# Attention on one core: part of the turning of probabilities by DMA, a paced TensorE order, and paired low products

## The chip, the cores and the metric

The kernel runs on one core of one Trainium2 chip, in one launch. The metric is the time of that launch on the device in microseconds (us), the median of several runs; less is better.

## The reference, cut to what matters

A trunk of two layers over 2048 tokens of width 1024, batch 1, in float32: a Mamba-2 mixer, then multi-head latent attention (16 heads; queries and keys of 64 + 32 columns, values of 64), then a final norm. The change touches the attention:

```python
for i in range(S // Q_BLOCK):                       # 16 query tiles of 128
    q0 = i * Q_BLOCK
    kv_len = q0 + Q_BLOCK
    s = einsum('bqhd,bkhd->bhqk', q_nope[:, q0:kv_len], k_nope[:, :kv_len]) + \
        einsum('bqhr,bkr->bhqk', q_rope[:, q0:kv_len], k_rope[:, :kv_len])
    mask = (q0 + local)[:, None] >= arange(kv_len)[None, :]
    p = softmax(where(mask, s * scale, -inf), axis=-1)
    outs.append(einsum('bhqk,bkhd->bqhd', p, v[:, :kv_len]))
```

The query and its scale, the shared keys and values, the gate and the output projection are computed around it.

## The kernel before

The kernel works in stages: the Mamba layer and the projections for the attention (to about 2127 us of the profiled execution), the attention (`heads`, to about 3050 us), and the gate, output projection and final norm (`back`, to the end). To keep float32's precision, a matrix is split into a high and a low part and multiplied in several passes: `mm3` (lines 84 to 87) is three TensorE passes, high by high, high by low, low by high.

**Attention.** The work is a list of 64 jobs, 16 heads by 4 blocks of 512 queries (`qb`, called block below). A block has four query tiles `j` of 128. For a query tile, `scores` cuts the keys up to the diagonal into chunks of at most 512 (`cuts`), so a tile of block 3 has four chunks. One chunk is one score step: `mm3` into a bank of PSUM (tag "mm", four banks), on the last chunk the mask (line 905), then VectorE's maximum of the bank (line 906). When all chunks of the tile are there, line 910 makes the negative row maximum `nm`, and ScalarE takes the exponential of each bank into a tile `Pr` in SBUF, with the row sum (line 918). The exponentials are held back in a list `late`: one is issued ahead of each following score step, and each frees a score bank. The two parts of all scores of a head are 40 chunks.

**Turning and values.** The value product needs the probabilities with the keys on the partitions. A unit is one key tile of 128 keys against the 512 queries of a block. `turn` transposes its four 128x128 squares on TensorE (line 933) into a bank with tag "tr", and `pair16` (lines 116 and 117) takes the bank, scaled by `PSCALE`, into a 16-bit high part (ScalarE) and a 16-bit low part (VectorE), both in a tile `PTs`. `values` multiplies them with the values (lines 943 and 944): the value tile has 128 columns, 64 of high parts and 64 of low ones, so both products give 64 rows of high and 64 of low, which `finish` adds when it stores them: rows 0 to 63 are written to `o_d` by SP's queue and rows 64 to 127 added by POOL's. On the diagonal, units are narrower (512, 384, 256 and 128 queries).

**Order.** TensorE's order in `heads` is the order in which the code issues it (a manual schedule). After the first `LAG` = 20 score steps, each score step is followed by the turns (T) and value products (V) that a hand-written table `CREDIT` gives for its block, query tile and chunk. The other engines' orders are made by the scheduler when the kernel is built, and each engine then works through its own queue in order; POOL's queue holds the loads of queries, keys and values (lines 833 to 847) and the accumulating stores (line 956), SP's holds the plain stores (line 952).

**Memory.** `Pr` has 24 buffers. The loads of a later head's queries and values wait for a buffer of the tag "xT". `back` prepares its output weights per step k (line 1016 a rounded copy on ScalarE, line 1017 the remainder on POOL); for k = 2 to 5 they have memory of their own, so that this is done while the attention still runs.

Of the kernel before, what the change touches and what calls it, by code (L numbers as in the profile page):

```python
# [40 lines left out]
LAG = 20  # L41
DEPTH = 2
CREDIT = (
    (("VT",), ("TV",), ("VT",), ("TV",)),
    (("", "VTVT"), ("", "TTVV"), ("", "TTVV"), ("", "TTVV")),
    (("TT", "", "VVTV"), ("TV", "", "VTTV"), ("TV", "", "TTVV"), ("TTV", "", "TVV")),
    (("T", "", "", "VVTTVTV"), ("T", "V", "", "VTTVTV"), ("T", "V", "V", "TVTTV"), ("TV", "V", "", "TVTVT")),
)
MAGIC = 12582912.0
PSCALE = 32768.0  # L50
# [18 lines left out]
class Net:  # L69
# [44 lines left out]
    def pair16(self, hi, lo, src, scale=1.0):  # L114

        self.nc.scalar.activation(hi, src, AF.Copy, scale=scale)  # L116
        self.nc.vector.scalar_tensor_tensor(lo, src, scale, hi, ALU.mult, ALU.subtract)  # L117
# [146 lines left out]
    def value_scale(self):  # L264
# [4 lines left out]
        for n in range(2):  # L269
# [18 lines left out]
            v.tensor_scalar(e, e, -25, None, ALU.add)  # L288
# [574 lines left out]
    def heads(self, sp):  # L863
        nc, v = self.nc, self.nc.vector
        begun = []
        keys, vals, quer = self.keys, self.vals, self.quer

        def cuts(kv):

            out, at = [], 0  # L870
            while at < kv:
                w = min(TB, kv - at)
                if kv - at == TB + P:
                    w = 384
                out.append((at, max(w, 256)))
                at += w
            return out

        def scores(h, qb, st):
# [8 lines left out]
            for j in range(4):  # L888
# [3 lines left out]
                mx = self.t(sp, "mx", [P, 4], bufs=4)  # L892
                banks = []
                for n, (c0, w) in enumerate(parts):
# [6 lines left out]
                    if n == nb - 1:  # L901
                        if qb == j == 0:
# [3 lines left out]
                    v.tensor_reduce(mx[:, n:n + 1], s[:, :w], AX.X, ALU.max)  # L906
                    banks.append((s, w))
                    yield CREDIT[qb][j][n]
                nm = self.t(sp, "nm", [P, 1], bufs=4)
                v.tensor_reduce(nm, mx[:, :nb], AX.X, ALU.max, negate=True)  # L910
# [4 lines left out]
                def exp(n, j=j, nb=nb, parts=parts, banks=banks, nm=nm, p=p, sm=sm):  # L915
                    s, w = banks[n]
                    x = self.t(sp, "Pr", [P, TB], bufs=NP)
                    nc.scalar.activation(x[:, :w], s[:, :w], AF.Exp, bias=nm, accum_out=sm[:, n:n + 1])  # L918
                    for c in range(0, w, P):
                        p[(parts[n][0] + c) // P] = x[:, c:c + P]  # L920
# [7 lines left out]
        def turn(h, qb, kb, st):  # L928
# [6 lines left out]
            u = self.t(sp, "PTs", [P, 2, TB], F16, bufs=5)  # L935
            self.pair16(u[:, 0, c], u[:, 1, c], pt[:, c], PSCALE)
            return u[:, :, c], c

        def values(h, qb, kb, st, u, c):
            if kb == 0:  # L940
                st["O"] = self.t(self.pp, "tr", [P, TB], bufs=4)
            nk = 4 * qb + 4
            nc.tensor.matmul(st["O"][:, c], vals[h][:, kb, :], u[:, 0], start=kb == 0, stop=False)  # L943
            nc.tensor.matmul(st["O"][:, c], vals[h][:, kb, :], u[:, 1], start=False, stop=kb == nk - 1)  # L944
            if kb == nk - 1:
# [22 lines left out]
        states = [{"P": []} for _ in jobs]  # L968
        sums = {}
        def ahead():  # L970
            for n, (h, qb) in enumerate(jobs):
                if qb == 0:
                    sums[h] = self.t(sp, "sum", [P, 16], bufs=3)
                yield from scores(h, qb, states[n])

        units = [(h, qb, kb, states[n]) for n, (h, qb) in enumerate(jobs) for kb in range(4 * qb + 4)]
        held = []

        def work(what):

            if what == "T" and units:
                a = units.pop(0)
                held.append((a, turn(*a)))
            elif what == "V" and held and (len(held) > DEPTH or not units):
                a, (u, c) = held.pop(0)
                values(*a, u, c)

        step = 0
        for credit in ahead():
            step += 1  # L990
            if step > LAG:
                for what in credit:
                    work(what)
        while units or held:
            work("T")
            work("V")
# [193 lines left out]
```

## Time and profile before

| | |
|---|---|
| median of 3 runs | 3239.51 us (3238.54 to 3240.34) |
| the profiled execution, its own time | 3238.15 us |
| its span (first to last instruction) | 3236.3 us |
| TensorE busy | 3156.2 us, 98% of the span |
| VectorE (DVE) busy | 2593.4 us, 80% |
| ScalarE (ACT) busy | 2055.2 us, 64% |
| GpSimd (POOL) busy | 646.2 us, 20% |
| mean granted TensorE clock | 0.995 |

The times of single instructions come from one profiled execution. Busy time counts the stretches in which an engine has an instruction on record; records of neighbours overlap by a little (a pipeline's tail), so an instruction's mean time is longer than the distance to the next one. PE is TensorE, PEld its weight load. In the profile's groups, "L117 DVE ... PTs<-tr,PTs" is line 117 on VectorE, writing tile PTs from tiles tr and PTs, with shapes, count, total and mean time, and the engine's idle time just ahead, with what ended it. The chain of waits follows the end back to what released each step; its pieces are a start, a time and a step, and "x8" means eight instructions merged.

### The profile page before, as it was taken

The page shows a single profiled execution, that of the slowest core. Times are in us where ns is not written, and L with a number is a line of the kernel's source. Part 1 is how long each engine was busy: PE and PEld are TensorE (multiplying, and loading weights), DVE is VectorE, ACT ScalarE, POOL GpSimd, SP SyncE. Part 2 cuts the span into 40 slices and gives each one's busy share as a digit, 9 for nine tenths or more (in the row PEclk, how much of TensorE's full clock was granted, in tenths as well). Part 3 has the DMA queues.
Part 4 walks back from the last instruction along what each step waited for, and adds up shares of the span by engine and source line. Part 5 has one row for each costly group of instructions (what it writes and reads, how often), then busy time and mean ns, then how long its engine had stood idle before and what let it go on. Part 6 is the DMA issues. An engine that isn't in the chain of part 4 may idle for free.

```text
span 3236.3 us, 50476 instructions
## 1 busy us (share of the span) xinstructions
PE 3156.2 (98%) x16708; PEld 2563.4 (79%) x16708; DVE 2593.4 (80%) x5490; ACT 2055.2 (64%) x5117; POOL 646.2 (20%) x842
## 2 busy tenths in 40 slices
PE   8999999999999999998999999999999999999998
PEld 6788888888888888887888888777777777777787
DVE  6988888889889888887776765668888888888675
ACT  5666666666657655666555554567777877778522
POOL 1221122221212222222211211222212212223100
PEclk9999999999999999999999999999999999999999
DMA  5333343333433334333466666753443434344385
GB/s 174 108 104 92 118 131 119 105 96 122 140 96 109 90 125 145 104 94 111 132 221 212 236 204 208 246 137 79 82 89 77 97 77 88 77 90 116 81 272 172
DMA packets 210572, 418.91 MB, mean 129 GB/s; under 512 B 27107, under 2 KB 68835, under 8 KB 208869
## 3 DMA queue, kind: packets, MB, share of 16 engines
q1 hardware_dynamic: 168900, 291.39, 28.9%
q0 software_dynamic: 41408, 124.29, 15.7%
q8 instruction: 132, 2.16, 0.3%
q14 instruction: 132, 1.07, 0.1%
HBM read 321.33 MB, written 94.24 MB: 128 GB/s over the span
## 4 chain that ended last, share of the span: by engine, by line
PE 44%; ACT 3%; DMA 2%; DVE 2%; issue 1%; SPq 0%; POOL 0%; ACTq 0%; DVEq 0%
PE mm L85 7%; PE mm L87 7%; PE mm L86 7%; PE tr L933 6%; PE tr L943 3%; PE tr L944 3%; PE tr L86 3%; PE tr L87 3%; PE tr L85 3%; ACT Pr L918 1%; DVE PTs L117 1%; ACT PTs L116 1%; DMA wraw<-in_kv_w_up_dram 1%; PE mm L905 1%; DMA wraw<-in_kv_w_down_dram 0%
## 5 line engine op out<-in xcount | busy, mean ns | idle before, releaser
L117 DVE SCALAR_TENSOR_TENSOR PTs<-tr,PTs 128x512 f16<-128x512 f32 (+3 forms) x640 | 374.7, 607 | 92.6 <-ACT PTs L116 86.0
L116 ACT ACTIVATE PTs<-tr 128x512 f16<-128x512 f32 (+3 forms) x640 | 328.2, 541 | 140.9 <-PE tr L933 140.0
L906 DVE TENSOR_REDUCE mx<-mm 128x1 f32<-128x512 f32 (+2 forms) x631 | 375.5, 607 | 45.4 <-PE mm L87 42.8
L918 ACT ACTIVATE Pr<-mm,nm 128x512 f32<-128x512 f32 (+2 forms) x631 | 395.1, 635 | 23.1 <-DVE nm L910 21.5
L108 ACT ACTIVATE wsp<-wraw 128x512 fp32r<-128x512 f32 (+1 forms) x452 | 251.1, 574 | 171.7 <-PE mm L87 82.4
L109 DVE TENSOR_TENSOR wsp<-wraw,wsp 128x512 fp32r<-128x512 f32 (+1 forms) x452 | 301.8, 680 | 69.7 <-ACT wsp L108 68.9
L85 PE MATMUL mm<-xT,wsp 128*128 128x512 f32 x800 | 321.0, 401 | 0.0
L933 PE MATMUL tr<-pack,Pr 128*128 128x128 f32 x2176 | 317.5, 273 | 0.9 <-ACT Os L950 0.8
L87 PE MATMUL mm<-xT,wsp 128*128 128x512 f32 x800 | 314.1, 393 | 0.0
L86 PE MATMUL mm<-xT,wsp 128*128 128x512 f32 x800 | 312.9, 391 | 0.0
L85 PE MATMUL mm<-K,xT 96*128 96x512 f32 (+2 forms) x639 | 286.7, 449 | 23.1 <-ACT Pr L918 21.7
L933 PEld LDWEIGHTS tr<-pack,Pr 128*128 128x128 f32 x2176 | 253.4, 141 | 49.3 <-ACT Os L950 1.6
L85 PE MATMUL mm<-wsp,xT 128*128 128x512 f32 (+1 forms) x640 | 242.1, 378 | 0.0
L86 PE MATMUL mm<-wsp,xT 128*128 128x512 f32 (+1 forms) x640 | 237.7, 371 | 0.0
L87 PE MATMUL mm<-wsp,xT 128*128 128x512 f32 (+1 forms) x640 | 237.5, 372 | 0.0
L87 PE MATMUL mm<-K,xT 96*128 96x512 f32 (+2 forms) x639 | 231.4, 362 | 0.0
L358 DVE SCALAR_TENSOR_TENSOR cacc<-craw,pack,cacc 128x512 f32<-128x512 f32 x288 | 216.5, 774 | 18.3 <-ACT cacc L356 17.8
L86 PE MATMUL mm<-K,xT 96*128 96x512 f32 (+2 forms) x639 | 231.1, 362 | 0.0
L496 POOL TENSOR_TENSOR Xp<-Xw,Xp 128x512 fp32r<-128x512 f32 x64 | 83.1, 1298 | 697.5 <-ACT Xp L495 393.1
L943 PE MATMUL tr<-PTs,xT 128*128 128x512 f16 (+3 forms) x640 | 222.0, 348 | 0.1
L538 ACT ACTIVATE Xw<-tr,d_wend 128x64 f32<-128x64 f32 x512 | 182.8, 358 | 58.7 <-DVE Xd L534 58.6
L944 PE MATMUL tr<-PTs,xT 128*128 128x512 f16 (+3 forms) x640 | 219.4, 347 | 0.0
(368 smaller groups left out, 8145.9 us busy)
## 6 DMA issues: line engine op xcount, KB each, us to landing
wraw<-in_ssm_w_in_dram SPq DMA_DIRECT2D x256, 256.0 KB, 2.8
big<-cumT SPq DMA_DIRECT2D x64, 512.0 KB, 4.0
wraw<-in_ssm_w_out_dram SPq DMA_DIRECT2D x128, 256.0 KB, 2.6
wraw<-in_ssm_w_in_dram SPq DMA_DIRECT2D x129, 128.0 KB, 2.2
xT<-qn_d POOLq DMA_DIRECT2D x64, 256.0 KB, 4.4
K<-kn_d POOLq DMA_DIRECT2D x15, 1024.0 KB, 9.2
wraw<-in_mla_w_uq_dram SPq DMA_DIRECT2D x36, 256.0 KB, 4.0
hx<-in_x_dram SPq DMA_DIRECT2D x16, 512.0 KB, 4.2
```

Source lines behind the costliest of these rows:

```text
L85: mm(out, l_hi, r_hi, start=start, stop=False)
L86: mm(out, l_hi, r_lo, start=False, stop=False)
L87: mm(out, l_lo, r_hi, start=False, stop=stop)
L108: nc.scalar.activation(hi, src, AF.Copy)
L109: nc.vector.tensor_tensor(lo, src, hi.bitcast(F32), ALU.subtract)
L116: self.nc.scalar.activation(hi, src, AF.Copy, scale=scale)
L117: self.nc.vector.scalar_tensor_tensor(lo, src, scale, hi, ALU.mult, ALU.subtract)
L906: v.tensor_reduce(mx[:, n:n + 1], s[:, :w], AX.X, ALU.max)
L918: nc.scalar.activation(x[:, :w], s[:, :w], AF.Exp, bias=nm, accum_out=sm[:, n:n + 1])
L933: nc.tensor.transpose(pt[:, j * P:(j + 1) * P], st["P"][j][kb], self.ident)
L943: nc.tensor.matmul(st["O"][:, c], vals[h][:, kb, :], u[:, 0], start=kb == 0, stop=False)
L944: nc.tensor.matmul(st["O"][:, c], vals[h][:, kb, :], u[:, 1], start=False, stop=kb == nk - 1)
```

## The change

- **Turning by DMA.** In blocks 1, 2 and 3 the first 1, 1 and 2 chunks of keys (`BYDMA`), all off the diagonal, aren't turned on TensorE. After the exponential, VectorE casts the 128x512 chunk to 16 bits, POOL subtracts for the low part, both into a tile `Ph` (four buffers), and SP issues one transposing DMA of the 128x1024 elements into `PX` (five buffers), from where the value products read.
- **Scale.** The factor 32768 goes into the exponential's bias (`PSHIFT` is its logarithm), and out of `pair16`, whose subtraction becomes a plain one. The maxima are taken negated, and `nm` is a running minimum: 28 small steps a head in place of 16. The first query tile of block 1 is cut 512 + 256, with a wider mask, in place of 384 + 256.
- **Low products.** `values` issues only the product with the high part. The low parts are collected, and `lows` multiplies four key tiles at a time: each with the 64 high columns of the values alone, key tiles in turn into rows 0 to 63 and 64 to 127 of the same bank.
- **Order.** `CREDIT` is replaced: each score step earns time for other work by its columns, 85% of it kept until the last chunk of a query tile, and `action` spends it by set prices. A job's turns and values start no sooner than `GAP` = 5 score steps after its last one; within a job, units turned by DMA and by TensorE are interleaved.
- **Memory.** The output weights of k = 2 to 5 move from their own pool into the pool of `back`, which lies where the attention's tiles were.

```diff
+BYDMA = (0, 1, 1, 2)
+T_US, V_US, S_US = 0.436, 0.216, 0.7
+L_US = 0.45
...
-    def pair16(self, hi, lo, src, scale=1.0):
-
-        self.nc.scalar.activation(hi, src, AF.Copy, scale=scale)
-        self.nc.vector.scalar_tensor_tensor(lo, src, scale, hi, ALU.mult, ALU.subtract)
+    def pair16(self, hi, lo, src):
+
+        self.nc.scalar.activation(hi, src, AF.Copy)
+        self.nc.vector.tensor_tensor(lo, src, hi, ALU.subtract)
...
-                    v.tensor_reduce(mx[:, n:n + 1], s[:, :w], AX.X, ALU.max)
+                    m = mx[:, n:n + 1]
+                    v.tensor_reduce(m, s[:, :w], AX.X, ALU.max, negate=True)
...
+                    if nb == 1:
+                        v.tensor_scalar(nm, m, PSHIFT, None, ALU.add)
+                    elif n == 1:
+                        v.scalar_tensor_tensor(nm, m, mx[:, 0:1], shift, ALU.min, ALU.add)
+                    elif n > 1:
+                        v.scalar_tensor_tensor(nm, m, shift, old, ALU.add, ALU.min)
...
                     nc.scalar.activation(x[:, :w], s[:, :w], AF.Exp, bias=nm, accum_out=sm[:, n:n + 1])
+                    if n < BYDMA[qb]:
+
+                        u = self.t(sp, "Ph", [P, 2, TB], F16, bufs=4)
+                        v.tensor_copy(u[:, 0], x)
+                        nc.gpsimd.tensor_tensor(u[:, 1], x, u[:, 0], ALU.subtract)
+                        if j == 0:
+                            st["X"].append(self.t(sp, "PX", [P, 2, 4, TB], F16, bufs=5))
+                        d = st["X"][n].rearrange("p s k q -> p (s k) q")[:, :, j * P:(j + 1) * P]
+                        nc.sync.dma_start_transpose(d, u.rearrange("p s k -> p (s k)"))
...
-            u = self.t(sp, "PTs", [P, 2, TB], F16, bufs=5)
-            self.pair16(u[:, 0, c], u[:, 1, c], pt[:, c], PSCALE)
+            hi, lo = self.t(sp, "PTh", [P, TB], F16, bufs=5), self.t(sp, "PTl", [P, TB], F16, bufs=10)
+            self.pair16(hi[:, c], lo[:, c], pt[:, c])
...
-            nc.tensor.matmul(st["O"][:, c], vals[h][:, kb, :], u[:, 0], start=kb == 0, stop=False)
-            nc.tensor.matmul(st["O"][:, c], vals[h][:, kb, :], u[:, 1], start=False, stop=kb == nk - 1)
+            nc.tensor.matmul(st["O"][:, c], vals[h][:, kb, :], u[0], start=not st["done"], stop=False)
+            st["done"] += 1
+            st["lo"].append((kb, u[1], c))
+
+        def lows(h, qb, st):
...
+            for i, (kb, l, c) in enumerate(st["lo"]):
+                d = slice(i % 2 * 64, i % 2 * 64 + 64)
+                nc.tensor.matmul(st["O"][d, c], vals[h][:, kb, 0:64], l, start=False, stop=end and i >= n - 2)
...
+            if owed and (len(owed[0][2]["lo"]) >= 4 or owed[0][2]["done"] == 4 * owed[0][1] + 4):
...
+                lows(h, qb, st)
+                return L_US * pairs
...
+            if turns and turns[0][0] < limit and (len(turned) <= DEPTH or not ready):
+                b = turns.pop(0)[1]
+                turned[b[:3]] = turn(*b)
+                return T_US * (4 - max(b[2] - 4 * b[1], 0)) / 4
...
+            limit = max([k + 1 for k in ended if k < n and ended[k] + GAP <= step], default=0)
+            if step <= LAG:
+                continue
+            share = 1.06 * rate * w
+            kept += share if last else share * 0.85
+            if last:
+                allowed, kept = allowed + kept, 0.0
+            else:
+                allowed += share * 0.15
+            while allowed > 0:
+                t = action(limit)
+                if not t:
+                    allowed = min(allowed, 2.0)
+                    break
+                allowed -= t
...
-                    W.append(self.t(self.wo, "W", [P, 2, 2, TB], F32R, bufs=4))
+                    W.append(self.t(sp, "W", [P, 2, 2, TB], F32R, bufs=4))
```

More of the change, by code (lines that the diff above doesn't have):

```diff
@@ L988, in heads, with order @@
-        step = 0
-        for credit in ahead():
-            step += 1
[L991 to L996, printed above, removed]
+                for step in scores(h, qb, states[n]):
+                    yield (n, *step)
+        def order(qb):
+            d, p = list(range(4 * BYDMA[qb])), list(range(4 * BYDMA[qb], 4 * qb + 4))
+            return sorted(d + p, key=lambda kb: kb / len(d) if kb in d else (kb - len(d) + 0.5) / len(p))
```

80 lines of the change are left out of this document (51 added, 29 removed).

## The prediction

> **What bounds the kernel now.** I read the page's first part first, then windows over the attention, then who waited for whom there, then the chain of waits, and last single groups by shape.
>
> ```profile
> PE 3156.2 (98%) x16708; PEld 2563.4 (79%) x16708; DVE 2593.4 (80%) x5490; ACT 2055.2 (64%) x5117; POOL 646.2 (20%) x842
> ```
>
> TensorE is busy 98% of the span, so only work taken off it, or idle time put on it, moves the end. The change lies in the attention. The window here starts and ends at the same instruction of the same step, 13 heads apart.
>
> ```profile
> core 0: us, PE busy (x) PEld busy (x) DVE busy (x) ACT busy (x) POOL busy (x), PEclk, DMA share, GB/s
> 2180.50:2922.00 741.50, 724.94 (x4589) 556.98 (x4587) 624.01 (x1483) 586.82 (x1625) 156.36 (x247) 1.00 0.43 85
> ```
>
> Divided by 13, one head takes 57.04 us: PE busy 55.8, DVE 48.0, ACT 45.1, POOL 12.0, the DMA engines 0.43 x 57.04 = 24.5. PE is the bound, idle 1.3 us a head, and the clock is full. DVE is only 8 us behind it.
>
> ```profile
> POOL xT L845 <- PE tr L962: 187.2, 14, 13.6
> ACT PTs L116 <- PE tr L933: 126.5, 126, 2.3
> DVE mx L906 <- PE mm L87: 35.5, 69, 1.2
> PE mm L85 <- ACT Pr L918: 17.7, 17, 1.2
> ```
>
> PE waits for one thing only: a score bank that the exponential has not yet emptied (17.7 us in 14 heads). All others wait for PE, and POOL can stand 13.6 us at one query load. How PE comes to wait is seen at the one stall of the head that starts at 2237.6:
>
> ```profile
> 2264.93 0.46 ACT Os L950
> 2265.43 0.60 ACT PTs L116
> 2266.06 1.29 DVE PTs L117 x2
> 2267.45 0.79 ACT Pr L918 x2
> 2268.28 0.50 PE mm L85
> ```
>
> Four instructions of two other engines, each in its queue's order, stand between PE and its bank.
>
> **The change part by part, per head.** What each PE step costs stands in the chain, where PE is back to back:
>
> ```profile
> 2237.59 0.88 PE tr L933 x8
> 2238.47 0.21 PE tr L943
> 2238.68 0.22 PE tr L944
> 2239.33 0.24 PE mm L85
> 2239.57 0.23 PE mm L86
> 2239.80 0.23 PE mm L87
> ...
> 2258.48 0.33 PE tr L933 x3
> 2258.92 0.20 PE tr L962
> ```
>
> *Transposes.* A head has 40 key tiles: 24 whole ones off the diagonal and 16 on it, worth 24 + 4 x 2.5 = 34 whole ones. Sixteen of the 24 now go by DMA (4 chunks of 4 tiles). Each had four transposes of 0.88 / 8 = 0.11: 16 x 4 x 0.11 = 7.0 us off PE.
>
> *Low products.* The second product costs 0.216 for each of 34 tiles, 7.3 us. If two at 64 output rows run side by side it is 3.7. The trace has no such pair; its bounds are 0 and 3.7 saved. Leaving the full array has a price near at hand: the 16-column transpose of L962 took 0.20 where its neighbours took 0.11, so 0.09 for going and coming back. The low products come in groups of four tiles: 1 + 2 + 3 + 4 = 10 groups, 0.9 us. I take 3.7 - 0.9 = 2.8, because the two halves write different rows and read different weights. The Trainium skill speaks for and against this (TensorEngine Tiling (Array Packing), Key Properties): tiles run in parallel, but changing the mode drains TensorE.
>
> ```profile
> L944 PE MATMUL tr<-PTs,xT 128*128 128x512 f16 x405 | 153.5, 379 | 0.0
> ```
>
> What a full drain would be, the row bounds: a product is on record for 0.379 and the next starts after 0.216, so 0.16 is hidden tail. Twenty changes would be 3.3 us and leave 0.4 of the gain. L962 showed less, so I stay with 0.9.
>
> *Padding and small parts.* The first query tile of block 1 now scores 512 + 256 keys, not 384 + 256: 128 / 512 x 0.70 = 0.18, and 0.07 for the wider mask. PE's own need is then 55.8 - 7.0 - 2.8 + 0.2 = 46.2 us.
>
> *The other engines.* For each of 16 chunk rows ACT loses a high copy, and DVE a subtraction; DVE gains a cast, POOL a subtraction, SP a transposing DMA.
>
> ```profile
> L117 DVE SCALAR_TENSOR_TENSOR PTs<-tr,PTs 128x512 f16<-128x512 f32 x404 | 270.3, 687 | 68.5 <-ACT PTs L116 62.5
> L918 ACT ACTIVATE Pr<-mm,nm 128x512 f32<-128x512 f32 x359 | 246.0, 694 | 15.9 <-DVE nm L910 14.4
> L906 DVE TENSOR_REDUCE mx<-mm 128x1 f32<-128x512 f32 x360 | 245.1, 685 | 38.0 <-PE mm L87 36.6
> L116 ACT ACTIVATE PTs<-tr 128x512 f16<-128x512 f32 x403 | 232.0, 600 | 81.6 <-PE tr L933 80.8
> L645 DVE CAST sz<-yt 128x512 f32<-128x512 int32 x4 | 1.7, 421 | 0.6 <-DMA yt<-in_positions_dram 0.6
> L496 POOL TENSOR_TENSOR Xp<-Xw,Xp 128x512 fp32r<-128x512 f32 x64 | 83.1, 1298 | 697.5 <-ACT Xp L495 393.1 <-issue 194.2 <-PE tr L87 70.1
> ...
> 2240.28 0.14 DVE L910 TENSOR_REDUCE nm<-mx 128x1 f32<-128x2 f32 x1
> 2240.34 1.15 DVE L906 TENSOR_REDUCE mx<-mm 128x1 f32<-128x512 f32 x2
> ```
>
> Two L117 in a row took 1.29 in the stall above, so one occupies DVE for 0.60. DVE: -16 x 0.60, +16 casts of 0.42 (the CAST row, also from SBUF to SBUF), and the running minimum makes 28 small steps where 16 were, +12 x 0.06 (2240.28 to 2240.34): -9.6 + 6.7 + 0.7, so 45.8. Were the cast as slow as a product of two tensors (0.69), 50.1. ACT: 16 high copies less, 600 ns each on record: at least 35.5, out of the way. POOL: 16 x 1.30 = 20.8, so 33. `tensor_tensor` in place of the scaled form: nothing, the read of PSUM is the same.
>
> *The DMA.* No transposing DMA is in the trace. Each moves 128 x 1024 x 2 bytes, 256 KB.
>
> ```profile
> wraw<-in_ssm_w_in_dram SPq DMA_DIRECT2D x256, 256.0 KB, 2.8
> hx<-in_x_dram SPq DMA_DIRECT2D x16, 512.0 KB, 4.2
> xT<-v_d POOLq DMA_DIRECT2D x16, 512.0 KB, 6.6
> ```
>
> From 256 to 512 KB the landing grows by 1.4, so a plain 256 KB occupies the engines for 1.4 us and lands in 2.8. The load of V, in pieces of 256 bytes, takes 2.4 more than a plain 512 KB, so 1.2 more for 256 KB: 2.6 to occupy, 4.0 to land. A transpose moves rows of 256 bytes too, but within SBUF. I take 1.7: 16 x 1.7 = 27 + 24.5 = 52 us of DMA a head; bounds 1.0 (less than plain, as no HBM is read) and 2.6 (66 us). The Trainium skill gives 261 GB/s for a transposing DMA, and 350 to 400 where contiguous (DMA: Bandwidth & Descriptors, Latency and other measured facts). By my estimate from that page it is 1.0 us each, and the DMA total would be 41 us; no run here shows it.
>
> *What is given back.* With less to interleave, PE meets the bank wait more often. From the last score of a query tile to the first free bank: hidden tail 0.16, reduction 0.69, minimum 0.14, exponential 0.69, 1.7 us. The work that PE has in between now averages 34 x (0.44 + 0.43) / 16 = 1.85 us a tile. After: high products 7.3, low 4.5, transposes 18 x 0.44 = 7.9, together 19.7, or 1.23 a tile. The pacing goes by columns, so block 3 with 43% of them has 2.1 a tile, of which 85% (1.8) stands behind the last score: level with 1.7. Block 2 has 1.3 and one spare bank of 0.70, block 1 0.8 and two. That leaves margins of 0.1 to 0.5, and DVE near full puts about one instruction (0.60) ahead of the reduction, ACT half of one (0.3). I take 0.5 us lost at each of the 12 tiles of blocks 1 to 3, 6.0 a head; bounds 0 and 0.9 x 16 = 14. That is the widest term.
>
> *Late chunks.* A job's values start no sooner than five score steps after its last. The last chunk row needs exponential 0.69, cast 0.42, subtraction 1.30 and landing 2.8 to 4.0: 5.2 to 6.4, against five steps of 53 / 40, 6.6 us, less as the steps of the next block 0 are short. I take 1.0 a head for it, bounds 0 and 4.
>
> *Sum.* 46.2 + 6.0 + 1.0 = 53.2, which is 3.8 less than 57.04; times 16, 61 us. After the last score the last job's first value waits for its chunk, some 4 us that backlog covers in part: +4.
>
> ```profile
> L1017 POOL TENSOR_TENSOR W<-wr,W 128x1024 fp32r<-128x1024 f32 x4 | 9.7, 2477 | 0.9 <-ACT W L1016 0.9
> ```
>
> The output weights of k = 2 to 5 move to memory that the attention holds until its end: a copy and POOL's 2.5 us come later, hidden behind k = 0 and 1 (2 x 8 x 0.70 = 11 us of PE). Uncovered, 3 to 4 us. The profiled execution took 3238.15 us, its span 3236.3; the median 3239.51 lies 1.4 above. 3238 - 61 + 4 = 3181, and 3182 on the median's footing.
>
> **The rivals.**
> *The transposing DMA sets the pace (slower).* The place: four Ph buffers. The cast waits for a free one, and behind the cast DVE's queue holds the reductions that free the score banks. It decides where 24.5 + 16 d passes 57, d = 2.0 us. For it: V's 256-byte pieces gave 2.6. Against it: that load reads HBM, this does not. At d = 2.3 a head takes 61.3: +4.3 x 16 = +69, 3308; at 2.6, +9.1 x 16, 3385.
> *POOL blocked.* The subtraction stands behind a query load that waits up to 13.6 us for the last head's values. If the four rows of block 1 wait that long against 6 us of cover, up to 7 us of PE return each head: 53.2 + 3 to 7, 3230 to 3294. Against it: the order on POOL follows a schedule in which both appear.
> *The low products do not overlap, or every change drains.* PE needs 2.4 to 3.7 more, partly in time that it would wait anyway: +1.5 to 3.7 a head, 3206 to 3241. The page's drain gives 2.4 of this.
> *Nothing is given back.* The fill covers every chain: 47.5 a head with today's idle, 3239 - 16 x 9.5 = 3087. Against it: PE waits already with 1.85 us of fill a tile.
>
> **How the numbers follow.** My forecast, 3182 with 3130 to 3225 of its own, 0.50; low products worth nothing 0.12; nothing given back 0.08; POOL blocked 0.10; DMA the pace 0.20. A measurement tells 0.2%, 6.5 us, from no change. Faster: 0.50 + 0.08 + 0.10 of the low products' case + a third of POOL's, less 0.07 for the open upper ends, 0.64; same 0.05; slower 0.31. The range reaches down past the forecast's own end into the full gain, and up through POOL's case: 3118 to 3290, leaving out most of the DMA rival and the full gain.
>
> **What would show it.** Right: L933 with 1152 transposes in place of 2176 (18 of 34 left); low products in pairs that start together, 0.43 to 0.47 for four; windows of 52 to 54 us a head with PE busy 46 to 47 and its idle put down to the exponential. Wrong: a transposing DMA that lands after over 5 us, or DVE casts waiting for it; POOL subtractions over 2 us; idle PE before the value products of a chunk; low products 0.2 us apart.

## Result: slower by 3.1%

The changed kernel took 3340.52 us (median of 4 runs, 3329.89 to 3345.80), the kernel before beside it 3239.03 (4 runs, 3236.62 to 3240.34). The ratio is 1.031, with an interval of 1.0284 to 1.0337. The profiled execution took 3342.15 us, its span 3340.4. The forecast was 3182 and faster.

The busy times of the page, first part, first engine line:

```profile
PE 3126.0 (94%) x15684; PEld 2440.6 (73%) x15684; DVE 2650.7 (79%) x5683; ACT 1947.6 (58%) x4861; POOL 942.5 (28%) x1098
```

TensorE has 30 us less busy time in a span that is 104 us longer. The windows over 13 heads, from one load of K to the same load 13 heads on:

```profile
core 0: us, PE busy (x) PEld busy (x) DVE busy (x) ACT busy (x) POOL busy (x), PEclk, DMA share, GB/s
2188.51:3014.73 826.22, 702.00 (x3780) 455.94 (x3776) 670.61 (x1647) 501.57 (x1423) 397.38 (x458) 0.94 0.87 144
```

Divided by 13, a head takes 63.6 us where it took 57.04. PE is busy for 54.0 of them (55.8 before) and idle for 9.6 (1.3), VectorE is busy for 51.6, POOL for 30.6, the DMA engines for 0.87 x 63.6 = 55.3 (24.5). The granted clock is 0.94, where it was 1.00. PE's waits in that stretch:

```profile
PE mm L85 <- ACT Pr L928: 97.5, 107, 3.8
PE tr L961 <- DMA PX<-Ph: 19.9, 6, 5.7
PE tr L961 <- issue: 3.9, 1, 3.9
```

The wait at the score banks, 1.2 us a head before (14.5 us in 12 heads), is now 97.5 / 13 = 7.5, and single waits reach 3.8 us. A second kind is new, high products (L961) that wait for a chunk turned by DMA: 23.8 / 13 = 1.8 a head. How the longest of these came about (timeline, most rows left out):

```profile
2600.50 0.42 DVE L932 CAST Ph<-Pr 128x512 f16<-128x512 f32 x1
2602.29 0.86 POOL L985 DMA_DIRECT2D o_d<-Os  x1 [8.77 <-DMA o_d<-Os]
2602.89 1.44 POOL L933 TENSOR_TENSOR Ph<-Pr,Ph 128x512 f16<-128x512 f32 x1
2604.36 1.24 SPq L937 DMA_TRANSPOSE PX<-Ph  x1
2609.46 0.58 PE L961 MATMUL tr<-PX,xT 128*128 128x512 f16 x1 [5.74 <-DMA PX<-Ph]
```

The cast was done at 2600.92, but POOL stood for 8.77 us at its accumulating store (L985), so that the subtraction behind it in the queue started 2.0 us late; from issue to landing it then took 5.0 us. At the wait that ends at 2860.63 the same store holds the subtraction up by 3.6 us. In the 13 heads POOL stands 181 us at this store, up to 9.9 at a time, and never over 2.1 at a query load.

What was added shows in the groups of that stretch (POOL's subtraction, VectorE's cast and the two forms of the running minimum); the transposing DMAs issued from 2180 to 3150 land after 4.1 us in the median:

```profile
L933 POOL TENSOR_TENSOR Ph<-Pr,Ph 128x512 f16<-128x512 f32 x209 | 256.6, 1243 | 230.8 <-DVE Ph L932 182.2 <-DVE sum L941 40.1 <-DMA o_d<-Os 4.0
L932 DVE CAST Ph<-Pr 128x512 f16<-128x512 f32 x208 | 120.9, 583 | 45.9 <-ACT Pr L928 22.7 <-issue 22.5
L917 DVE SCALAR_TENSOR_TENSOR nm<-mx,shift 128x1 f32<-128x1 f32 x156 | 62.6, 401 | 0.3
L919 DVE SCALAR_TENSOR_TENSOR nm<-mx,shift,nm 128x1 f32<-128x1 f32 x156 | 44.7, 287 | 1.4
```

A minimum over 128 x 1 elements takes 0.29 to 0.40 us in the mean (0.21 in the median), a cast 0.58; both were put lower. Of the 384 minima of the whole run that read two tensors 62 take over 0.3 us, and 59 of these end within 0.12 us of the end of a subtraction on POOL. One stall of the changed kernel shows how they get there (timeline, all engines, most rows left out; the bracket is the idle time before an instruction and what ended it):

```profile
2417.93 0.39 PE L86 MATMUL mm<-K,xT 96*128 96x512 f32 x1
2418.16 0.40 PE L87 MATMUL mm<-K,xT 96*128 96x512 f32 x1
...
2419.22 1.02 DVE L909 TENSOR_REDUCE mx<-mm 128x1 f32<-128x512 f32 x2
2419.82 2.50 POOL L933 TENSOR_TENSOR Ph<-Pr,Ph 128x512 f16<-128x512 f32 x2
2420.16 2.20 DVE L919 SCALAR_TENSOR_TENSOR nm<-mx,shift,nm 128x1 f32<-128x1 f32 x1
2422.28 0.68 DVE L117 TENSOR_TENSOR PTl<-tr,PTh 128x512 f16<-128x512 f32 x1
2422.88 0.20 DVE L919 SCALAR_TENSOR_TENSOR nm<-mx,shift,nm 128x1 f32<-128x1 f32 x1
...
2423.12 0.69 ACT L928 ACTIVATE Pr<-mm,nm 128x512 f32<-128x512 f32 x1 [1.60 <-DVE nm L919]
...
2423.95 0.80 PE L85 MATMUL mm<-K,xT 96*128 96x512 f32 x1 [3.12 <-ACT Pr L928]
...
2424.54 0.63 PE L86 MATMUL mm<-K,xT 96*128 96x512 f32 x1
2424.97 0.63 PE L87 MATMUL mm<-K,xT 96*128 96x512 f32 x1
```

The minimum reads two tensors from SBUF. It starts while POOL subtracts, and ends at 2422.36, when POOL's two subtractions end (2422.32). Then a subtraction of VectorE's own (L117) stands ahead of the last minimum. The first exponential starts 2.9 us after the reductions, and PE stands for 3.12 us. After that, products of 512 columns last 0.63 us and start 0.43 apart; before the stall they lasted 0.39 and started 0.23 apart: half the clock. The Trainium skill (SBUF — State Buffer, "SBUF: two separate sides") says that VectorE and GpSimd share one pair of ports as an exclusive lock, held for a whole instruction; the trace agrees, 2.20 us for a step of 0.2.

The windows over the first part of this stall and the time behind it, and over a shorter wait of 1.67 us (2224.74 to 2226.41) and the time behind that:

```profile
2420.83:2422.58 1.75, 0.00 (x0) 0.00 (x0) 1.75 (x2) 0.68 (x2) 1.75 (x4) 1.00 0.71 143
2422.58:2429.41 6.83, 5.46 (x13) 3.77 (x14) 4.93 (x10) 2.57 (x8) 3.88 (x5) 0.50 1.06 188
2224.61:2228.02 3.41, 1.74 (x9) 1.31 (x8) 2.41 (x8) 2.44 (x8) 1.57 (x4) 1.00 1.10 188
2228.02:2231.43 3.41, 3.41 (x15) 2.65 (x14) 2.55 (x8) 0.62 (x2) 2.95 (x4) 0.50 1.20 139
```

The clock (third number from the end) falls 1.75 us into the stall, and it falls after the shorter wait too. In the clock records of these 13 heads there are 18 stretches at half clock, of 3.41, 6.83 or 10.24 us, 95.5 us in all; in 13 heads of the kernel before there is none. The Trainium skill (TensorE: Matmul & The Clock Gate, "What's actually happening") says that an idle window of about 3.4 us takes the clock to half; here single waits of 1.4 to 1.9 us were enough, so on this point the measurement decides.

### The profile page after: what moved, and what is told of

It reads as the page before. It is cut to its first block, busy times and chain, and to the rows that moved or that the text cites. A ratio compares the mean times of both kernels' runs of the same rounds, so it can differ in the third digit from the quotient of the medians.

```text
span 3340.4 us, 49591 instructions
## 1 busy us (share of the span) xinstructions
PE 3126.0 (94%) x15684; PEld 2440.6 (73%) x15684; DVE 2650.7 (79%) x5683; ACT 1947.6 (58%) x4861; POOL 942.5 (28%) x1098
## 5 line engine op out<-in xcount | busy, mean ns | idle before, releaser
L85 PE MATMUL mm<-K,xT 96*128 96x512 f32 (+2 forms) x639 | 297.3, 465 | 121.4 <-ACT Pr L928 120.3
L933 POOL TENSOR_TENSOR Ph<-Pr,Ph 128x512 f16<-128x512 f32 x256 | 312.1, 1233 | 309.9 <-DVE Ph L932 256.1
L116 ACT ACTIVATE PTh<-tr 128x512 f16<-128x512 f32 (+3 forms) x384 | 182.6, 490 | 250.0 <-PE tr L952 248.2
L85 PEld LDWEIGHTS mm<-K,xT 96*128 96x128 f32 x639 | 127.9, 200 | 226.1 <-ACT Pr L928 194.8
L117 DVE TENSOR_TENSOR PTl<-tr,PTh 128x512 f16<-128x512 f32 (+3 forms) x384 | 207.0, 552 | 70.2 <-ACT PTh L116 67.7
L86 PE MATMUL mm<-K,xT 96*128 96x512 f32 (+2 forms) x639 | 243.9, 382 | 0.0
L87 PE MATMUL mm<-K,xT 96*128 96x512 f32 (+2 forms) x639 | 243.6, 381 | 0.0
L85 PE MATMUL mm<-wsp,yT 128*128 128x512 f32 x512 | 207.6, 410 | 3.6 <-ACT wsp L111 3.3
L86 PE MATMUL mm<-wsp,yT 128*128 128x512 f32 x512 | 204.6, 400 | 0.6 <-DVE wsp L112 0.6
```

The source lines that it names most:

```text
L85: mm(out, l_hi, r_hi, start=start, stop=False)
L86: mm(out, l_hi, r_lo, start=False, stop=False)
L87: mm(out, l_lo, r_hi, start=False, stop=stop)
L116: self.nc.scalar.activation(hi, src, AF.Copy)
L117: self.nc.vector.tensor_tensor(lo, src, hi, ALU.subtract)
L933: nc.gpsimd.tensor_tensor(u[:, 1], x, u[:, 0], ALU.subtract)
```

## The experiments

Three theories: **A**, VectorE held by POOL's subtraction, and the half clock after it; **B**, the transposing DMA; **C**, the chain from the last score of a query tile over maximum, minimum and exponential to the free bank, which TensorE's work no longer covers. The kernel before took 3240.9 to 3244.9 us beside all these runs; single runs are given as one time. The four runs of the changed kernel lie up to 16 us apart, so a single run that differs from it by less shows no difference.

**1. Parts of the change alone.** The low products in pairs, in the kernel before, whose order stays as written by hand (the scaled pair, W and the rest too):

```
-  matmul(st["O"][:, c], vals[h][:, kb, :], u[1], ...)
+  st["lo"].append((kb, u[1], c))
+  if kb % 4 == 3:
+      for i, (k, l, e) in enumerate(st["lo"]):
+          d = slice(i % 2 * 64, i % 2 * 64 + 64)
+          matmul(st["O"][d, e], vals[h][:, k, 0:64], l, ...)
```

> The kernel before, with its hand-written order, and only the low products changed: after every fourth unit the four low products are issued in pairs. By the first set of runs theory C has become the first: the computed order alone, without DMA, costs some 90 us. If that is so, the hand-written order keeps TensorE as busy as before and the pairs save 1.7 to 2.8 us a head, 3195 to 3213 us. If instead the paired products are what costs (a change of the array's mode that holds TensorE up), 3240 to 3300.

3292.71 us, slower by 52. Windows over 12 heads and one group of four in the timeline; PE's only wait in them is the one for a score bank, 33.3 us, 0.9 at most:

```profile
2239.25:2962.22 722.97, 686.65 (x4236) 480.08 (x4236) 575.06 (x1369) 542.31 (x1501) 144.40 (x229) 1.00 0.41 81
```

```profile
2252.13 0.59 PE L943 MATMUL tr<-PTh,xT 128*128 128x512 f16 x2
2252.65 0.62 PE L948 MATMUL tr<-PTl,xT 128*64 128x512 f16 x4
2253.20 0.50 PE L85 MATMUL mm<-K,xT 96*128 96x512 f32 x1
2253.54 0.40 PE L86 MATMUL mm<-K,xT 96*128 96x512 f32 x1
```

The four products start 0.09 us late (2 x 0.216 after 2252.13 is 2252.56), the next score 0.12 later than without a change of mode (0.43 after 2252.65), and that score takes 0.34 to the next product's start where its neighbours take 0.23. So this group costs 0.43 + 0.32 = 0.75 against 0.86 and gains 0.11; ahead of transposes a full group gains 0.16. The four groups of a head on the diagonal, whose products have 512, 384, 128 and 256 columns, gain next to nothing: their second pair starts 0.24 us after the first, as in a full group, though the first has 512 and 384 columns in place of 512 and 512. Over all groups of the 12 heads the pairs gain about 0.7 us a head, not the 2.8 of the forecast. Yet a head takes 60.25 us, 3.2 more than before, at full clock and without any DMA or POOL work. The bank waits grew from 1.2 to 2.8 us a head, and PE's busy time from 55.8 to 57.2.

The computed order without the DMA and with full-width products, the minimum taken by one reduction and one addition:

```
-BYDMA = (0, 1, 1, 2)
+BYDMA = (0, 0, 0, 0)
-T_US, V_US, S_US = 0.436, 0.216, 0.7
-L_US = 0.45
+T_US, V_US, S_US = 0.436, 0.432, 0.7
+L_US = 0.0
```

> The computed order alone: no DMA, both value products at full width right after each other, the row maximum by one reduction. Theory C: TensorE waits for its banks and for the turned units as without DMA before, and has 3 us a head more to do than there, 3340 to 3390 us. If the order is harmless and the paired products cost the time: 3235 to 3260.

3368.46 us, slower by 127; it has one small step more in the chain, so that not all of this is the order. Order, pairs and running minimum together, `BYDMA` zero and nothing else undone:

> No chunk goes by DMA; the computed order, the single-input scale, the running minimum and the paired low products stay. TensorE needs 2.8 us a head less than the kernel before. Theories A and B: with neither GpSimd's subtraction nor the transposing DMA the low products' gain shows, 3190 to 3215 us. Theory C: idle at the score banks of 3 us a head or more eats it, 3235 to 3300.

3328.16 us. Without any transposing DMA and at a clock of 1.00 these parts make 87 us; the whole change makes 101. Neither A nor B can be the reason, since nothing here is subtracted on POOL or turned by DMA. That it is C is argued: of the 5.3 us that a head is longer, waits of PE show 2.6, and the rest is on record as busy time.

**2. The port and POOL.** The minimum by one reduction and one addition of a constant, each with one tensor input:

```
+  v.tensor_reduce(mn, mx[:, :nb], AX.X, ALU.min)
+  v.tensor_scalar(nm, mn, PSHIFT, None, ALU.add)
```

> The row maximum of a query tile is made by one reduction over its negated chunk maxima and one addition of the constant, both with a single tensor input, in place of the running minimum with two. Theory A (VectorE and GpSimd hold each other up: a VectorE step with two SBUF inputs waits until GpSimd's subtraction is over, and the minimum is on the chain that frees score banks): no minimum over 0.3 us, and most of the 47 us of excess time that the minima have now returns, 3280 to 3300 us. Theory B (the transposing DMA keeps the four Ph buffers, and the casts waiting for them hold VectorE's queue): within 15 us of 3340. Theory C (the order leaves too little work for TensorE behind the last score of a query tile, whatever the rest does): within 15 us of 3340.

3373.12 us, 33 slower than the change. The small steps fell to 0.15 us each, but the chain has one step more for each of 256 tiles. POOL's subtraction left out (the low half is a constant):

```
-  u = self.t(sp, "Ph", [P, 2, TB], F16, bufs=4)
+  u = fixed[0]; fixed.append(fixed.pop(0))
   v.tensor_copy(u[:, 0], x)
-  nc.gpsimd.tensor_tensor(u[:, 1], x, u[:, 0], ALU.subtract)
```

> GpSimd's 256 subtractions are left out: the low halves of four fixed Ph tiles are zero throughout, so the low part of the probabilities turned by DMA is missing from the result; casts, DMA, and products are all still made. Theory A: minima at 0.2 us and casts at 0.43 us throughout, 3240 to 3275 us. Theory B: the DMA moves as much and each chunk is only 1.2 us earlier, 3310 to 3335. Theory C: 3310 to 3335.

3300.12 us, 40 less than the change. A is worth no more than this by this cut, which also makes each chunk ready earlier. Casts fell to 0.43 us and the two minima to 0.21, so it was the subtraction that held them. The longest bank wait fell to 1.6 us, and the clock rose to 0.96 only. All VectorE instructions with one tensor input, and the cast on ScalarE:

```
-  v.scalar_tensor_tensor(nm, m, mx[:, 0:1], shift, ALU.min, ALU.add)
+  v.tensor_scalar(nm, m, mx[:, 0:1], PSHIFT, ALU.min, ALU.add)
-  v.tensor_copy(u[:, 0], x)
+  nc.scalar.activation(u[:, 0], x, AF.Copy)
```

> The running minimum is taken with tensor_scalar (the other operands as scalars), and the cast from float32 to float16 runs on ScalarE, so that no VectorE instruction of the chunk path reads two tensors or goes from SBUF to SBUF beside POOL's subtraction; all else as in the changed kernel. Theory A (VectorE held by POOL's subtraction, then half clock): minima of 0.06 to 0.2 us, no stall of PE over 3 us, clock back above 0.98, 3280 to 3305 us. Theories B (the transposing DMA) and C (nothing covers the chain from score to bank): 3325 to 3350.

3349.07 us. The minima took 0.21 us each, but a bank wait still reached 5.7 us: now the cast stands in ScalarE's queue, ahead of exponentials, and waits for a Ph buffer (22.8 us in 2180 to 3000). The same with eight Ph buffers:

> The changed kernel with A and B both taken away as far as buffers can: one-input minima and the cast on ScalarE, and eight Ph buffers in place of four (20 Pr in place of 24), so that the cast does not wait in ScalarE's queue for a transposing DMA. Theories A and B together: 3240 to 3290, no wait of PE over 3 us. Theory C: 3325 to 3350.

3324.72 us, the longest bank wait 1.5 us. With A gone and the buffers' part of B with it, 82 of the 101 us are left, and 81.4 us of bank waits between 2180 and 3000 (95.7 in the change between 2190 and 3000).

**3. The DMA.** Eight Ph buffers in the changed kernel, 20 Pr in place of 24:

> Eight Ph buffers in place of four (and 20 of Pr in place of 24), so that casts wait less for a transposing DMA to land. Theory B: 3290 to 3315 us, with VectorE's casts no longer held. Theories A and C: within 15 us of 3340.

3349.78 us: more buffers gain nothing here. Half the transposed bytes, so that the low products read the high part:

```
-  nc.sync.dma_start_transpose(d, u.rearrange("p s k -> p (s k)"))
+  nc.sync.dma_start_transpose(st["X"][n][:, 0, :, j * P:(j + 1) * P], u[:, 0])
```

> Only the high half of a chunk is transposed by DMA (128 x 512 in place of 128 x 1024), and the low products of these key tiles read the high part once more, so that part of the result is not the reference's; GpSimd's subtraction is still made. The DMA engines' share in the attention falls from 0.87 to about 0.65. Theory B: landing under 3.5 us, no value product that waits for a chunk, 3240 to 3280 us. Theory A: minima and casts as long as now, 3310 to 3335. Theory C: 3310 to 3335.

3310.44 us, 30 less. The DMA share fell to 0.67, the landing to 2.7 us, the waits for chunks vanished, and the waits at the banks (99.3 us in 2190 to 3000) stayed. So half of B's bytes, and with them all waits for chunks, are worth 30.

**4. The order by hand, with the DMA.** The table of before in place of the computed pace, its "T" of a tile turned by DMA left empty:

> The changed kernel with DMA, subtraction and paired low products, but TensorE's order by the hand-written table of the kernel before, in which the turns of units that come by DMA are left out, so that all work stays 20 score steps behind. Theory C alone (order): 3160 to 3220 us, with TensorE idle under 4 us a head. Theories A and B (the other engines and the DMA hold the banks whatever the order): 3290 to 3340, with waits for the exponential as long as in the changed kernel but none of TensorE for a chunk.

3329.86 us, 11 less than the change and as long as its fastest run: the pacing rule alone is not what was wrong, as A and B expected. From there the pairs out too, minima with one input, and the cast on ScalarE, so that of the change the DMA is left (with its running minimum):

> The kernel before's hand-written order, its full-width low products, the one-input minima and the cast on ScalarE; what is left of the change is the chunks that are turned by DMA (16 x 0.44 = 7.0 us of TensorE a head less). Theory C: the 7.0 come back as waits at the score banks, 3215 to 3260 us. If the order, the pairs and the port were the whole loss: 3125 to 3170. Theory B (the DMA itself costs): 3280 to 3320, with DMA near 0.9 busy and TensorE waiting for chunks.

3346.09 us. Only block 3 by DMA (`BYDMA = (0, 0, 0, 2)`):

> As the kernel with the transposing DMA alone (hand-written order, full-width low products), but only block 3's two chunks go by DMA, where the fill was widest: 8 of 24 tiles, 3.5 us of TensorE a head less. If the fill of block 3 covers the chain: 3180 to 3205 us. Theory C: 3225 to 3250. Theory B: DMA falls to about 0.65 busy and the time lies within 15 of the kernel before.

3301.38 us. PE's waits, 2180 to 3000, of the first:

```profile
PE mm L90 <- ACT Pr L931: 84.1, 116, 5.3
PE tr L964 <- DMA PX<-Ph: 31.1, 5, 9.5
PE tr L964 <- issue: 17.8, 3, 7.1
```

In the second they are 41.1 at the banks and 29.2 for chunks. There the DMA share is 0.69, and yet most of the chunks that PE waits for land about 9 us after their issue. For these two no expectation held, neither C's, B's nor "the rest was the whole loss". The DMA alone costs as much as the whole change, 101 us, and with half of the chunks 56; both contain the running minimum, which costs 42 by itself (experiment 7).

**5. Does TensorE's work set the time?** Each transpose that is left is issued twice into the same bank:

```
+  for _ in range(2):
       nc.tensor.transpose(pt[...], st["P"][j][kb], self.ident)
```

> Every transpose that is left on TensorE is issued twice into the same bank: 18 x 0.44 = 7.9 us of TensorE work a head more, 127 us in all, and nothing else changed, the order neither. If TensorE's work sets the time: 3440 to 3470 us. Theory C (TensorE waits for the chain anyway, and work that is put in only fills the wait): 3330 to 3375, with the waits at the score banks down by about as much as the work is up.

3363.54 us, as C expected: 127 us of TensorE work cost 23. The window from 2190 to 3000:

```profile
2190.00:3000.00 810.00, 743.99 (x4580) 528.28 (x4579) 644.84 (x1590) 487.83 (x1380) 387.37 (x444) 0.98 0.88 142
```

The bank waits halved (45.5 us over 13 heads), and the clock went from 0.94 to 0.98, since work now lies where stalls were. So most of the added work was free. That taking more work off would not have helped either is inferred from this, not tried.

**6. The chain taken away.** The exponentials take a constant (and a scale of 0.001) in place of the row maximum; maxima and minima are still computed, but nobody waits for them. First in the changed kernel, then in the kernel before:

```
-  nc.scalar.activation(x[:, :w], s[:, :w], AF.Exp, bias=nm, ...)
+  nc.scalar.activation(x[:, :w], s[:, :w], AF.Exp, scale=0.001, bias=fix, ...)
```

> The changed kernel with exponentials that take a constant in place of the row maximum (and a scale of 0.001, so that they stay finite); maxima and running minima are all still computed, so every engine has the same instructions, but no exponential waits for them. The probabilities are other ones. Theory C (the chain sets the time): 3170 to 3230 us, bank waits under 30 us in the 14 heads, clock back near 1. Theories A and B: 3300 to 3345.

> The same edit in the kernel before: constant and scale in place of the maximum. Its bank waits were 17.7 us in 14 heads, so at most about 20 us can go: 3215 to 3240 us, by every theory.

3261.61 and 3211.59 us. Windows over 12 heads of each, and in between PE's waits for chunks and for banks in the first:

```profile
2182.64:2883.48 700.84, 616.69 (x3486) 421.49 (x3484) 591.70 (x1524) 462.92 (x1317) 367.93 (x423) 0.94 1.00 155
```

```profile
PE tr L963 <- DMA PX<-Ph: 35.4, 12, 6.8
PE tr L963 <- issue: 20.5, 4, 8.9
PE mm L85 <- ACT Pr L930: 8.5, 7, 4.3
```

```profile
2225.77:2891.08 665.31, 665.03 (x4239) 518.69 (x4237) 572.71 (x1369) 558.25 (x1503) 144.70 (x229) 1.00 0.44 88
```

Without the chain the kernel before is bound by TensorE to the last tenth of a per cent (665.03 of 665.31), 31 us faster, more than the 20 us of waits that its profile showed. The changed kernel falls by 79 us, with its bank waits nearly gone as C expected. So C is worth 79 - 31 = 48 of the difference of 101 by this cut. But the time met neither range, and the clock stayed at 0.94: a head still takes 58.4 us, and PE waits for chunks. What the other 50 us are is not settled. The DMA share of 1.00 doesn't show engines that are always busy. It adds up packet times, which overlap: over pieces of 5 us of this stretch it reads 0.22 to 2.36, and for 12% of the stretch no packet is under way. Transposing DMAs land 5.2 us after their issue in the median, but up to 20.7, and POOL stands up to 10.7 us at its accumulating store, ahead of subtractions. The same edit in the kernel with the DMA alone:

> The same edit in the kernel with the transposing DMA alone (hand-written order, full-width low products), which took 3346. Theory C: 3160 to 3220. Theory B (chunks that come late, DMA near 0.95 busy): 3290 to 3345.

3263.72 us, 82 less, at a DMA share of 1.07. The time is the same, but the wait is another: PE stands 79.9 us at transposes, in 14 pieces of up to 10.2 (2190 to 3000), while ScalarE's casts, ahead of the high copies in its queue, wait for a Ph buffer (106.8 us).

**7. What lengthens the chain.** The running minimum alone, in the kernel before:

```
-  v.tensor_reduce(mx[:, n:n + 1], s[:, :w], AX.X, ALU.max)
+  v.tensor_reduce(m, s[:, :w], AX.X, ALU.max, negate=True)
+  nm = m if n == 0 else min(m, nm)      # tensor_scalar
-  v.tensor_reduce(nm, mx[:, :nb], AX.X, ALU.max, negate=True)
```

> The kernel before with one edit: the maximum over the parts of a row is taken as a running minimum of negated maxima, with tensor_scalar, in place of one reduction at the end. The step in the chain falls from 0.15 to about 0.06 us, and DVE has 12 small steps a head more. Theory C: the bank waits of 20 us in all shrink by a third to a half, 3225 to 3235 us. If small DVE steps cost more than the chain gains: 3240 to 3255.

3282.72 us (4 runs), a ratio of 1.0128 with an interval of 1.0111 to 1.0145: 42 us slower, with TensorE's order untouched. It had been put down as a possible gain. The same query tile of the same block, timelines of the kernel before and of this one (PE's last score and its next, VectorE, the first exponential):

```profile
2340.97 0.23 PE L905 MATMUL mm<-mk,idb 128*128 128x128 bf16 x1
2341.24 0.69 DVE L906 TENSOR_REDUCE mx<-mm 128x1 f32<-128x512 f32 x1
2341.97 0.16 DVE L910 TENSOR_REDUCE nm<-mx 128x1 f32<-128x4 f32 x1
2342.24 0.68 ACT L918 ACTIVATE Pr<-mm,nm 128x512 f32<-128x512 f32 x1
2343.14 0.36 PE L85 MATMUL mm<-K,xT 96*128 96x256 f32 x1
```

```profile
2353.35 0.23 PE L905 MATMUL mm<-mk,idb 128*128 128x128 bf16 x1
2353.62 0.69 DVE L907 TENSOR_REDUCE mx<-mm 128x1 f32<-128x512 f32 x1
2354.23 0.20 DVE L913 TENSOR_SCALAR nm<-mx,nm 128x1 f32<-128x1 f32 x1
2354.75 0.69 DVE L117 SCALAR_TENSOR_TENSOR PTs<-tr,PTs 128x512 f16<-128x512 f32 x1 [0.32 <-ACT PTs L116]
2355.36 0.20 DVE L913 TENSOR_SCALAR nm<-mx,nm 128x1 f32<-128x1 f32 x1
2355.60 0.69 ACT L922 ACTIVATE Pr<-mm,nm 128x512 f32<-128x512 f32 x1
2356.43 0.39 PE L85 MATMUL mm<-K,xT 96*128 96x256 f32 x1 [0.67 <-ACT Pr L922]
```

Before, the exponential starts 1.27 us after the last score's start; now 2.25. The step itself grew by 0.05 us. The rest is VectorE's queue: between the last two minima stands a low subtraction that itself waited for ScalarE, 0.32 idle and 0.61 of work, while the last minimum had its input. In this tile, then, the small step was one more place in an in-order queue at which another tile's 0.6 us could stand.

Worked out from the traces tile by tile (224 tiles of the 14 middle heads): from the start of a tile's last maximum to the end of its first exponential, and how many VectorE instructions of over 0.25 us stand between maximum and minimum, and ScalarE instructions of that size between minimum and exponential (records overlap, so that these two counts are good to some tenths):

| kernel | us | VectorE | ScalarE |
|---|---|---|---|
| before | 1.97 | 0.43 | 0.54 |
| running minimum alone, blocks 2 and 3 | 2.16 (before 1.80) | 0.49 (0.23) | 0.30 (0.42) |
| pairs alone | 2.29 | 0.55 | 0.95 |
| order alone | 2.47 | 1.17 | 0.25 |
| changed | 2.26 | 0.53 | 0.38 |
| changed, minimum by a reduction and an addition | 2.52 | 0.96 | 0.34 |

In blocks 2 and 3 the running minimum adds 0.36 us to eight tiles, 2.9 us a head. In blocks 0 and 1 it takes 0.28 off (1.87 after 2.15), so that over all tiles the chain grew by 0.05 only. The head became 2.8 us longer, 717.56 / 12 = 59.80; that this is the 2.9 of the long tiles, while the short tiles' gain goes unused, is argued and not shown:

```profile
2235.82:2953.38 717.56, 679.13 (x4239) 515.47 (x4237) 598.45 (x1466) 546.28 (x1501) 144.54 (x230) 1.00 0.40 82
```

Then the other way, small steps taken out of the kernel before (block 0's tiles take the negated maximum as bias, and a block's row sums are added by one reduction in place of four):

```
-  nm = self.t(...); v.tensor_reduce(nm, mx[:, :nb], AX.X, ALU.max, negate=True)
+  if nb == 1: nm = mx[:, 0:1]           # else as it was
-  if n == nb - 1: v.tensor_reduce(sums[h][:, 4 * qb + j], sm[:, :nb], ...)
+  if j == 3 and n == nb - 1: v.tensor_reduce(sums[h][:, 4 * qb:4 * qb + 4], sm[:, :, :nb], ...)
```

> The kernel before with fewer small VectorE steps: block 0's query tiles, which have one part, take the negated maximum itself as the bias (4 steps of 0.15 us a head less, in the chain), and the row sums of a block are added by one reduction at its last tile instead of four (12 steps of 0.15 a head less, not in the chain but in VectorE's queue ahead of it). If the time follows the small steps as it did with the running minimum (2.6 us of VectorE a head gave 2.6 us): 16 x 0.15 x 16 = 38 less, but not below the 3212 of the run without any chain: 3212 to 3225. If only the chain's steps count: 4 x 0.15 x 16 = 10 less, 3229 to 3235. If neither: 3239 to 3245.

3239.28 us (11 runs) against 3241.97 (15), a ratio on record of 0.9995 with an interval of 0.9985 to 1.0004: no difference. That speaks against the number of small steps and against VectorE's busy time, and leaves what stands in the queue inside the chain of the long tiles. No version that beats the kernel before was found.

## Why the prediction was wrong

**What held.** 1152 transposes are left, POOL's subtraction took 1.24 us against 1.30, and the landing 4.1 us against 2.8 to 4.0. The two halves of a pair do start together:

```profile
2414.08 0.40 PE L972 MATMUL tr<-PX,xT 128*64 128x512 f16 x1
2414.09 0.40 PE L972 MATMUL tr<-PTl,xT 128*64 128x512 f16 x1
```

Even the widest term, 6.0 us a head at the score banks, came near: 7.5 (the sum starts from PE's busy time, so that the 1.2 of before are in it). This is partly luck. There are 8 waits of 0.9 us a head where 12 of 0.5 were forecast, and without POOL's subtraction, which the term did not have, a third of them goes (experiment 2).

**Step by step, a head.** The forecast of 53.2 was 46.2 of PE's own work, 6.0 at the banks and 1.0 for chunks. Measured are 54.0 of busy time, 7.5, 1.8 and 0.3 of other waits: 63.6. So the step that failed most is *"PE's own need is then 55.8 - 7.0 - 2.8 + 0.2 = 46.2 us"*, which makes 7.8 of the 10.4 us. Of these, 2.1 are the pairs, which gain 0.7 (experiment 1) where 2.8 stood. The clock makes 3.2, where the forecast had nothing: PE was busy for 82.8 of the 95.5 us at half clock, and half of that, 41.4 us in 13 heads, is lost. The other 2.5 stay open. A wait that is shorter than the 0.16 us tail of a product can't be told from work in these rows. That such waits exist the kernel before shows: with the same TensorE instructions, PE was busy for 55.4 us a head without the chain (665.03 / 12), 55.8 with it, and 56.6 with the running minimum (679.13 / 12). That they make all of the 2.5 is argued, not shown.

1. *"the clock is full"* was read from a kernel with few and short stalls, and carried over to one with many: 3.2 us a head. The order alone (experiment 1) idled for 5.0 us a head in waits of up to 1.4 us at a clock of 0.99, the change for 9.6 in waits of up to 5.7 at 0.94. Whether it is the length of the waits or their sum that counts, these runs don't separate.
2. *The low products.* The price of a change of mode was taken from one narrow transpose (0.09 for going and coming back), against the Trainium skill's rule that a change drains TensorE (TensorEngine Tiling (Array Packing), Key Properties). The group of experiment 1 pays 0.32, 0.16 each way, just the tail that the prediction had worked out from the row for this rule. Its estimate was that 0.4 us a head are left of the gain, the measurement 0.7, the forecast 2.8.
3. *The running minimum* was counted as 12 steps of 0.06 us on VectorE, 0.7 a head. By itself it cost 2.8 (experiment 7), as it seems through what it lets into the chain. This is the same loop that the prediction described for its given-back term, but there only TensorE's fill was counted as changing, and the chain's own 1.7 us were held fixed.
4. *VectorE and POOL together.* Casts and minima were priced from rows in which POOL was idle. Held by POOL's subtraction they took 0.58 and 0.29 to 0.40 in the mean. Left out, this is worth up to 40 us in all (experiment 2).
5. *The DMA and POOL's queue.* 1.7 us each made 52 us of DMA a head. By packet times it is (55.3 - 24.5) / 16 = 1.9 in the changed kernel and (58.4 - 24.5) / 16 = 2.1 without the chain, near the 2.0 from which the rival "the transposing DMA sets the pace" was to decide. The Trainium skill's 261 GB/s (DMA: Bandwidth & Descriptors, Latency and other measured facts) gave 1.0 by the prediction's estimate; the measurement decides. As packet times overlap, this sum is no floor under the head. What PE waits for is the single chunk: the sum for late chunks had five steps of cover and nothing for POOL's accumulating store, and it came to 1.8 where 1.0 stood. With the chain gone the change came to 3262, so that "nothing is given back", 3087, was out of reach even then.

The rivals: the DMA's price was near the mark, but with four Ph buffers or eight the change takes as long (experiment 3). "Every change drains" was nearly right, and makes a fifth of the miss. POOL is blocked, though not by the query load (2.1 us at most) but by the accumulating store; a kernel without this block was not tried.

**What stays open** is how 101 us divide: the parts don't add up. Order, pairs and running minimum without the DMA cost 87, the DMA with the running minimum 101, all together 101, as if the waits of one hid those of the other.

## What to carry to other kernels

An engine that is busy for 98% can still stand in a ring that runs at its length: before work is taken off it, double some of that work, and take the ring's dependence away, and see which of the two moves the time. A step in such a ring can cost what the in-order queues let stand ahead of it (0.9 us in the tile of experiment 7), not its own 0.06 to 0.2. Price transfers by when the single one lands, not by a mean share of the DMA engines, and look at what stands ahead of each step in its queue.

## Not expected of the hardware

- A VectorE step over 128 x 1 elements with two SBUF inputs took up to 3.3 us beside POOL subtractions of 1.2 us: the longest started during one and ended with the second one after it.
- Products at half the clock followed a stall of TensorE of 3.12 us, and single waits of 1.4 to 1.9 us as well; in all the granted clock over 13 heads was 0.94, and putting 127 us of repeated transposes into the stalls brought it to 0.98.
- A transposing DMA within SBUF (256 KB of 2-byte elements) added packet times of 1.9 to 2.1 us on each of the 16 DMA engines in the mean, where the prediction's estimate for a plain 256 KB that reads HBM was 1.4 us.
